# A two-layer FFN and mixer trunk: three pairs of hidden chunks per phase as block products, part of their weight sums by adding DMAs

## The chip, the cores and the metric

One core of a Trainium2 chip runs the whole program. The metric is the time of one execution in device microseconds, the median of several. TensorE (PE) multiplies, VectorE (DVE) and ScalarE (ACT) do the elementwise work, GpSimd (POOL) does little here, SyncE (SP) issues most DMAs.

## The reference

Two layers, each with a half-step FFN, a mixer (differential attention beside an mLSTM) and a second half-step FFN, each between two RMSNorms. x is 256 tokens by 1024, the hidden width is 2816. Only the FFN is touched:

```python
def _swiglu(h, w_in, w_out):
    gate, up = jnp.split(h @ w_in, 2, axis=-1)
    return (jax.nn.silu(gate) * up) @ w_out
...
h = _swiglu(_rmsnorm(x, g[0]), ffn_w_in[l, 0], ffn_w_out[l, 0])
x = x + 0.5 * _rmsnorm(h, g[1])
```

So there are six phases, FFN, mixer, FFN, FFN, mixer, FFN, and the four FFN phases multiply 256 x 1024 tokens by 1024 x 5632 weights and 256 x 2816 by 2816 x 1024, in float32.

## The kernel before, in words

**Precision.** A float32 product is made of three matmuls on fp32r operands (`mm3`, L504-508): high by high, high by low, low by high. A weight piece is one DMA of 128 x 2048 (1 MB, `fetch`, L283-289, on SP's queue) and is split in two halves of 128 x 1024: ACT casts the high part, DVE subtracts for the low part (`halved`, L291-301, the rows of L295 and L296). The raw tiles are three buffers and, every fourth time in an FFN, a shared one (wx); the split halves have seven buffers each, and three in ten borrow from another pool (`half_tiles`, L386).

**Chunks.** The hidden width is cut in 11 chunks of 256. An ordinary chunk (step I) takes two weight pieces and, for both token tiles, 4 x 3 matmuls per piece into one PSUM bank; SiLU and gate follow (`ffn_hidden`, L637), the hidden tile is turned by a transposing DMA on SP's queue (`ffn_planes`, L643, `ffn_joined`, L653) and split again (`ffn_hilo`, L675). Its output part (step O, `out_part`) adds into four PSUM banks that stay open over the phase.

**Pairs.** Step P takes two chunks at once (`pair`, from L764): the two token tiles, the two halves of the input rows and the gate and up columns of both chunks make 2 x 2 blocks, and the Strassen-Winograd scheme gets the block product from seven products of 12 matmuls each (`product`, L759-762) where eight would do it directly. The weight side of the seven products P1 to P7 comes from `pair_blocks` (L310-338): besides the four raw blocks b11, b12, b22, b21 it needs b11 + b12, that sum plus b22, b12 + b22, and the first sum plus b21. Each of the four sums is two DVE additions of 128 x 1024 (L322); every product's weights are split in two halves. The running sum sits in two tiles of the mixer, qk and wt (`spare`, L303). The token sums are made by `pair_tokens` (L341-384) in steps S0 to S2; in all phases but the first they start from scaled tokens that `prenorm_half` (L528) left in the same spare tiles.

**The last chunk** (I10) is computed turned (`in_turned`, L730-742, with `token_scales` and `ffn_turned`): weights stationary, tokens moving, so that its hidden layer comes out already turned.

**Order.** STEPS (L37) lists the steps of a phase after chunks 0 and 1: I a chunk's input, P a pair, S token sums, L the load of an output piece, O an output part. The order of the instructions on each engine is made by a scheduler from this order; `after` (L253) adds ties between instructions. At the phase's end ("ending") PE's order is fixed by hand: output parts 8, 9, 10 of token tile 0, then its postnorm, while token tile 1 follows.

Of the kernel before, what the change touches and what calls it, by code (L numbers as in the profile page):

```python
# [25 lines left out]
P = 128  # L26
# [10 lines left out]
STEPS = "I2 L1 S0 O0 I3 L2 S1 O1 S2 P4 L3 O2 L4 O3 I6 L5 O4 I7 L6 O5 P8 L7 O6 L8 O7 I10 L9".split()  # L37
# [22 lines left out]
def _pack(inp):  # L60
# [9 lines left out]
    def ffn(at, l, f):  # L70
        n = w_in[l, f].reshape(2, 4, P, 2, NC_FF, 256).transpose(0, 3, 2, 1, 4, 5)
        a = n.transpose(4, 0, 2, 3, 1, 5).reshape(NC_FF, 2, P, 2048)
        b = w_out[l, f].reshape(NC_FF, 2, P, D).transpose(0, 2, 1, 3).reshape(NC_FF, P, 2048)
        order = [a[0, 0], a[0, 1], a[1, 0], a[1, 1], b[0]]
        for step in STEPS:
            c = int(step[1:])
            if step[0] == "P":
                order += [n[kh, g, :, :, c:c + 2].reshape(P, 2048) for kh, g in ((0, 0), (0, 1), (1, 1), (1, 0))]
# [57 lines left out]
class _Trunk:  # L136
    def __init__(self, tc, a, out, pools):
        self.tc, self.nc, self.a, self.out = tc, tc.nc, a, out
        self.const, self.wr, self.wl, self.wh, self.tr, self.k2, self.k4, self.ded, self.hp, self.sm, self.ps = pools
        self.piece_at = 0  # L140
        self.parts = None
        self.raws, self.four = 0, False
        self.n = 0
        self.turns = []
        self.halves = 0
        self.both = [None, None]
        self.lend = True

# [161 lines left out]
    def pair_blocks(self):  # L310


        def fetch():
            raw = self.fetch()
            return [raw[:, j] for j in range(2)]

        def split(raw):
            return [self.halved(raw[j]) for j in range(2)]

        def add(out, a, b):  # L320
            for j in range(2):
                self.nc.vector.tensor_tensor(out[j], a[j], b[j], op=ALU.add)  # L322
# [12 lines left out]
        w["P2"] = split(b21)  # L335
        w["P3"] = split(b22)
        add(run, run, b21)
        w["P4"] = split(run)
        return w

    def pair_tokens(self, both, kept):  # L341
# [4 lines left out]
        two = self.t2("aT1", (P, 2, 4, P))  # L346
        s, low = two[:, 0], two[:, 1]
# [4 lines left out]
        def g(kh, t):  # L352
            return self.spare()[t][:, kh * 512:kh * 512 + 512].rearrange("p (k n) -> p k n", k=4)
# [150 lines left out]
    def mm3(self, ps, xh, xl, wh, wl, start, stop):  # L504
        mm = self.nc.tensor.matmul
        mm(ps, xh, wh, start=start, stop=False)  # L506
        mm(ps, xh, wl, start=False, stop=False)  # L507
        mm(ps, xl, wh, start=False, stop=stop)  # L508

# [18 lines left out]
    def prenorm_half(self, t, gi, hf):  # L528
# [4 lines left out]
        if gi % 3 == 1:  # L533
            xg = self.t2("xg", (P, 4, P))
        else:
            xg = self.spare()[t][:, hf * 512:hf * 512 + 512].rearrange("p (k n) -> p k n", k=4)
# [142 lines left out]
    def token_scales(self, r):  # L679

        nc = self.nc
        ptr = self.bank_tr((P, NT * P))
        for t in range(NT):
            nc.tensor.transpose(ptr[:, t * P:(t + 1) * P], r[t].broadcast_to([P, P]), self.ident)
        rows = self.const.tile([P, NT * P], F32, tag="rows", bufs=1, name=self.name("rows"))
        nc.scalar.activation(rows, ptr, AF.Copy)
        return rows

    def ffn_block(self, bank, rows):


        nc, n = self.nc, NT * P
        su = self.t2("su", (P, 2, n))
        for i in range(2):
            nc.scalar.activation(su[:, i], bank[i][:, n:2 * n], AF.Copy)
            nc.vector.tensor_tensor(su[:, i], bank[i][:, 0:n], su[:, i], op=ALU.add)
            nc.vector.tensor_tensor(su[:, i], su[:, i], rows, op=ALU.mult)
            if i == 0:
                self.func(su[:, 0], su[:, 0], AF.Silu)
        nc.vector.tensor_tensor(su[:, 1], su[:, 1], su[:, 0], op=ALU.mult)  # L700
        return su[:, 1].rearrange("p (t j) -> p t j", t=NT)

    def ffn_turned(self, banks, rows):


        ops = [self.ffn_operand() for _ in range(NT)]
        for j in range(2):
            h = self.ffn_block(banks[j], rows)
            for t in range(NT):
                self.guards = [self.ffn_hilo(h[:, t], *(v[:, j] for v in ops[t]))]  # L710
        return [[tuple(v[:, j] for v in ops[t]) for j in range(2)] for t in range(NT)]

    def ffn(self, pre, gi_post):
# [9 lines left out]
        def out_part(c, t, h, wo):  # L723
            for hf in range(2):
                for k in range(2):
                    self.mm3(po[t][hf], *h[t][k], *self.cols(wo, 2 * k + hf),
                             start=c == 0 and k == 0, stop=c == NC_FF - 1 and k == 1)

        def in_turned(banks, w, both):


            blocks = [(banks[j][i], slice(i * 256 + j * P, i * 256 + j * P + P)) for j in range(2) for i in range(2)]
            for group, khs in ((blocks, (0,)), (blocks[:2], (1,)), (blocks[2:], (1,))):
                for kh in khs:
                    for b, c in group:
                        for k in range(4):
                            self.nc.tensor.matmul(b, self.cols(w[kh], k)[0][:, c], both[kh][:, k].rearrange("p i t -> p (i t)"),  # L737
                                                  start=kh == 0 and k == 0, stop=False, skip_group_check=True)
                for b, c in group:
                    for kh in khs:  # L740
                        for k in range(4):
                            self.nc.tensor.matmul(b[:, 0:NT * P], self.cols(w[kh], k)[1][:, c], both[kh][:, k, 0:NT].rearrange("p i t -> p (i t)"),  # L742
                                                  start=False, stop=kh == 1 and k == 3, skip_group_check=True)
# [15 lines left out]
        def product(b, x, w, new):  # L759
            for k in range(4):  # L760
                for n, (st, mv) in enumerate(((x[0], 0), (x[0], 1), (x[1], 0))):
                    self.nc.tensor.matmul(b, st[:, k, :], self.cols(w, k)[mv], start=new and k == n == 0,  # L762
                                          stop=k == 3 and n == 2, skip_group_check=True)

        def pair(c):
# [3 lines left out]
            w = self.pair_blocks()  # L769
# [19 lines left out]
            product(b4, s4, w["P3"], False)  # L789
# [5 lines left out]
            product(b3, xT[1][1], w["P4"], False)  # L795
# [7 lines left out]
        def pair_ready(others):  # L803
            c, turned = sent.pop("pair")
            ops = [[self.ffn_operand() for _ in range(NT)] for _ in range(2)]
            for t in range(NT):
                h = self.ffn_joined(turned[t], others)
                others = [self.ffn_hilo(h[:, j], *ops[j][t])[0] for j in range(2)]
# [3 lines left out]
        hs, po, wo, sent = {}, [], {}, {}  # L812
# [50 lines left out]
        both, swap = list(self.both), 0  # L863
        tokens = self.pair_tokens(both, kept)
        for at, step in enumerate(STEPS):
            kind, c = step[0], int(step[1:])
            if kind == "P":
                pair(c)
                swap = 1
            elif kind == "S":  # L870
                sums = next(tokens)
            elif kind == "L":
                if wo.get(c) is None:
                    wo[c] = self.piece()
            elif kind == "I":
                if c == 3:
                    g = self.load_gpost(gi_post)
                    yield "middle"
# [3 lines left out]
                if "pair" in sent and c != END[-1]:  # L882
                    pair_ready([cut])
                for later in STEPS[at + 1:]:
# [3 lines left out]
                if c == END[-1]:  # L888
                    if "pair" in sent:
                        pair_ready([self.cut])  # L890
                    ready(c - 1, [self.cut])
                    break
                pins = [self.bank_pin() if swap else self.bank_tr() for _ in range(NT)]
                swap = 1 - swap
# [3 lines left out]
                chunk(c, pins)  # L898
            else:
# [578 lines left out]
```

## Time and profile before

| what | value |
|---|---|
| median of 3 runs | 940.26 us (939.74 to 940.84) |
| profiled execution | 940.3 us, span 938.5 us |
| DMA: mean, HBM read | 202 GB/s, 177.01 MB |
| share of the weight queue (q1) | 59.1% of 16 engines' span |
| PE on the chain that ended last | 99% |
| first DVE rows of L580 (postnorm) by phase | 173.9, 279.4, 460.5, 636.9, 742.5, 921.7 us |

A row of a group reads: line, engine, operation, written tile<-read tiles, shapes, count | busy us, mean ns of one | idle time of the engine just before, and who ended it. A row of the timeline reads: start, duration, engine, line, operation, count of merged instructions. A row of the windows reads: window, its length, busy us (and count) of PE, PE's weight loads, DVE, ACT and POOL, the granted clock, the DMA share and GB/s. A row of the waits reads: who <- whom: us in total, times, longest.

### The profile page before, as it was taken

What the parts mean: (1) busy time and instruction counts of PE and PEld (TensorE: products, weight loads), DVE (VectorE), ACT (ScalarE), POOL (GpSimd) and SP (SyncE); (2) the same over time, 40 slices, a digit from 0 to 9 for tenths busy, and PEclk for the clock granted to TensorE, in tenths of its full rate; (3) what the DMA queues carried; (4) which work ended last, traced back from release to release, by engine and by line L of the source; (5) the groups of instructions that cost most, each with busy time, mean ns of one, the idle gap of its engine ahead of it and who ended that gap; (6) DMA issues with size and microseconds to landing.
All of it is one profiled execution on the core that took longest, in us unless ns stands there. A gap on an engine that the chain in (4) does not pass through costs nothing.

```text
span 938.5 us, 12082 instructions
## 1 busy us (share of the span) xinstructions
PE 931.4 (99%) x4427; PEld 771.5 (82%) x4427; DVE 775.5 (83%) x1079; ACT 668.4 (71%) x1033; POOL 29.4 (3%) x57
## 2 busy tenths in 40 slices
PE   9999999999999999999999999999999999999997
PEld 7888888888888888888888888888888888888885
DVE  7989797889867899788698987968898588986974
ACT  8967786677856868676587865866778478766862
POOL 2000000000020000000000000000001100000000
PEclk9999999999999999999999999999999999999999
DMA  9957857346362866838468585473554348486531
GB/s 354 342 169 275 251 192 218 119 152 221 138 232 90 303 167 225 303 107 309 121 237 257 172 267 189 155 237 135 189 193 169 146 157 302 148 300 184 186 115 46
DMA packets 69882, 189.34 MB, mean 202 GB/s; under 512 B 45274, under 2 KB 46426, under 8 KB 49086
## 3 DMA queue, kind: packets, MB, share of 16 engines
q1 hardware_dynamic: 69246, 187.95, 59.1%
q8 instruction: 35, 0.57, 0.2%
q10 hardware_dynamic: 576, 0.61, 0.2%
q14 instruction: 25, 0.20, 0.1%
HBM read 177.01 MB, written 1.05 MB: 190 GB/s over the span
## 4 chain that ended last, share of the span: by engine, by line
PE 99%; DVE 0%; ACT 0%; POOLq 0%; DVEq 0%; issue 0%; ACTq 0%
PE pin L506 11%; PE pin L508 10%; PE pin L507 10%; PE bk L506 10%; PE bk L507 10%; PE bk L508 10%; PE ptr L762 9%; PE pin L762 7%; PE ptr L507 3%; PE ptr L506 3%; PE ptr L508 3%; PE ptr L737 2%; PE pin L737 2%; PE ptr L532 1%; PE ptr L1100 1%; PE pin L742 1%
## 5 line engine op out<-in xcount | busy, mean ns | idle before, releaser
L296 DVE TENSOR_TENSOR wl<-wr,wh 128x1024 fp32r<-128x1024 f32 x262 | 313.6, 1221 | 42.2 <-ACT wh L295 39.4
L295 ACT ACTIVATE wh<-wr 128x1024 fp32r<-128x1024 f32 x262 | 269.5, 1055 | 55.9 <-PE bk L508 15.8
L506 PE MATMUL pin<-wh,both 128*128 128x512 f32 x432 | 171.3, 399 | 0.0
L507 PE MATMUL pin<-wl,both 128*128 128x512 f32 x432 | 168.4, 390 | 0.0
L508 PE MATMUL pin<-wh,both 128*128 128x512 f32 x432 | 168.2, 390 | 0.0
L507 PE MATMUL bk<-wl,hh 128*128 128x512 f32 x352 | 136.3, 389 | 0.0
L506 PE MATMUL bk<-wh,hh 128*128 128x512 f32 x352 | 135.8, 390 | 0.0
L508 PE MATMUL bk<-wh,hl 128*128 128x512 f32 x352 | 133.4, 389 | 0.0
L508 PEld LDWEIGHTS pin<-wh,both 128*128 128x128 f32 x432 | 81.1, 188 | 17.4
L506 PEld LDWEIGHTS pin<-wh,both 128*128 128x128 f32 x432 | 81.3, 188 | 17.2 <-issue 0.7
L507 PEld LDWEIGHTS pin<-wl,both 128*128 128x128 f32 x432 | 81.3, 188 | 15.5
L295 ACT ACTIVATE wh<-wx 128x1024 fp32r<-128x1024 f32 x62 | 64.3, 1055 | 31.9 <-PE bk L508 10.2
L762 PE MATMUL ptr<-wh,both 128*128 128x512 f32 x256 | 84.0, 389 | 0.0
L296 DVE TENSOR_TENSOR wl<-wx,wh 128x1024 fp32r<-128x1024 f32 x62 | 74.7, 1220 | 10.2 <-ACT wh L295 9.5
L508 PEld LDWEIGHTS bk<-wh,hl 128*128 128x128 f32 x352 | 66.1, 188 | 13.8
L506 PEld LDWEIGHTS bk<-wh,hh 128*128 128x128 f32 x352 | 66.1, 188 | 13.5
L507 PEld LDWEIGHTS bk<-wl,hh 128*128 128x128 f32 x352 | 66.1, 188 | 13.4
L762 PE MATMUL pin<-wh,both 128*128 128x512 f32 x192 | 63.0, 389 | 0.0
L762 PEld LDWEIGHTS ptr<-wh,both 128*128 128x128 f32 x256 | 48.0, 188 | 10.0
L507 PE MATMUL ptr<-wl,both 128*128 128x512 f32 x128 | 49.8, 389 | 0.0
L508 PE MATMUL ptr<-wh,both 128*128 128x512 f32 x128 | 49.8, 389 | 0.0
L762 PE MATMUL ptr<-wl,both 128*128 128x512 f32 x128 | 49.8, 389 | 0.0
(263 smaller groups left out, 1464.2 us busy)
## 6 DMA issues: line engine op xcount, KB each, us to landing
wr<-in_w_dram SPq DMA_DIRECT2D x131, 1024.0 KB, 5.1
wx<-in_w_dram SPq DMA_DIRECT2D x31, 1024.0 KB, 5.0
gpost<-in_gpost_dram SPq DMA_DIRECT2D x6, 512.0 KB, 6.2
wr<-in_w_dram SPq DMA_DIRECT2D x2, 512.0 KB, 6.3
wr<-in_w_dram SPq DMA_DIRECT2D x3, 256.0 KB, 4.5
x<-in_x_dram SPq DMA_DIRECT2D x3, 256.0 KB, 5.2
h<-planes SPq DMA_TRANSPOSE x32, 3.3
out_dram<-x SPq DMA_DIRECT2D x2, 256.0 KB, 2.1
```

The costliest lines, as they stand in the source:

```text
L295: ia = nc.scalar.activation(hi, raw, AF.Copy)
L296: iv = nc.vector.tensor_tensor(lo, raw, hi.bitcast(F32), op=ALU.subtract)
L506: mm(ps, xh, wh, start=start, stop=False)
L507: mm(ps, xh, wl, start=False, stop=False)
L508: mm(ps, xl, wh, start=False, stop=stop)
L532: nc.tensor.transpose(ptr[:, k, :], x[:, (4 * hf + k) * P:(4 * hf + k + 1) * P], self.ident)
L737: self.nc.tensor.matmul(b, self.cols(w[kh], k)[0][:, c], both[kh][:, k].rearrange("p i t -> p (i t)"), start=kh == 0 and k == 0, stop=Fals ...
L742: self.nc.tensor.matmul(b[:, 0:NT * P], self.cols(w[kh], k)[1][:, c], both[kh][:, k, 0:NT].rearrange("p i t -> p (i t)"), start=False, sto ...
L762: self.nc.tensor.matmul(b, st[:, k, :], self.cols(w, k)[mv], start=new and k == n == 0, stop=k == 3 and n == 2, skip_group_check=True)
L1100: self.T(ptr[:, b, :], a[:, b * P:(b + 1) * P], self.tr.ident)
```

## The change

- A phase after the first now runs chunks 0, 1, 2, 5 and 8 as ordinary ones and the pairs 3+4, 6+7 and 9+10. The first phase runs chunks 0 to 3 and 6 to 8 as ordinary ones and the pairs 4+5 and 9+10. The turned form of the last chunk and its helpers are gone.
- A new step D starts a pair's first sum: GpSimd's queue copies b12 into the run tile and then adds b11 to it from HBM by an accumulating DMA, 2 x 512 KB each. Inside such a pair, b22 is added to the raw b12 tile in the same way. DVE keeps the other two sums. The pair 4+5 of the first phase has no D and keeps all four on DVE. A pair's pieces come in the order b12, b11, b22, b21.
- The run tiles are the spare ones for the D3 and D9 pairs and the scaled-token tiles for P6. The scaled tokens move to two other tiles: that of aT1, and the one that otherwise holds the post-norm gains. So the gains are loaded in a step of their own (G0), after P6.
- Token tile 1 of the output part three below a pair in the list (O6), and all of O7, are tied to come after the pair's last product. O7 moves to the phase's end. Product P4 is tied to come after P3.
- In the first phase the mixer's constants ("middle") are loaded after chunk 6; they were loaded before chunk 3.

```diff
-STEPS = "I2 L1 S0 O0 I3 L2 S1 O1 S2 P4 L3 O2 L4 O3 I6 L5 O4 I7 L6 O5 P8 L7 O6 L8 O7 I10 L9".split()
+FIRST_STEPS = "I2 L1 S0 O0 I3 L2 S1 O1 S2 P4 L3 O2 D9 L4 O3 I6 L5 O4 I7 L6 O5 G0 I8 L7 P9 L8 O6 L9".split()
+STEPS = "D3 I2 L1 S0 O0 S1 L2 O1 S2 D6 P3 L3 O2 D9 I5 L4 O3 P6 G0 L5 O4 L6 O5 I8 L7 P9 L8 O6 L9".split()
...
+    def by_dma(self, out, i, add=False):
+        for j, v in enumerate(out):
+            self.nc.gpsimd.dma_start(v, self.a["w"][i][:, j * 1024:j * 1024 + 1024], **(dict(accum_op=ALU.add) if add else {}))
+
-    def pair_blocks(self):
+    def pair_blocks(self, run):
...
-        b11, b12 = fetch(), fetch()
+        b12 = fetch()
+        if run:
+            self.by_dma(b12, self.piece_at + 1, True)
+        b11 = fetch()
         w = {"P1": split(b11)}
-        run = self.spare()
-        add(run, b11, b12)
+        summed = run is not None
+        if not summed:
+            run = self.spare()
+            add(run, b11, b12)
         w["P5"] = split(run)
         b22 = fetch()
         add(run, run, b22)
         w["P6"] = split(run)
-        add(b12, b12, b22)
+        if not summed:
+            add(b12, b12, b22)
         w["P7"] = split(b12)
...
+    def scaled_tile(self, t):
+        if t == 0:
+            return self.t2("aT1", (P, 1024))
+        return self.const.tile([P, 1024], F32, tag="gpost", bufs=1, name=self.name("xgt"))
...
-    def in_turned(banks, w, both):
...
+            elif kind == "D":
+                runs[c] = [v for v in self.scaled] if c == 6 else self.spare()
+                i = self.piece_at + sum({"P": 4, "I": 2, "L": wo.get(int(v[1:])) is None}.get(v[0], 0)
+                                        for v in steps[at + 1:steps.index(f"P{c}")])
+                self.by_dma(runs[c], i)
+                self.by_dma(runs[c], i + 1, True)
+            elif kind == "G":
+                g = self.load_gpost(gi_post)
...
-                pins = [self.bank_pin() if swap else self.bank_tr() for _ in range(NT)]
-                swap = 1 - swap
+                pins = [self.bank_tr() if c in (2, 7) else self.bank_pin() for _ in range(NT)]
...
-                    out_part(c, t, hs[c], wo[c])
-        rows = self.token_scales(r)
-        banks = [[self.bank_pin() for _ in range(2)], [self.bank_tr() for _ in range(2)]]
-        in_turned(banks, ws, both)
+                    out_part(c, t, hs[c], wo[c], ended.get(c + 3, []) if t else [])
+        wo[END[-1]] = self.piece()
+        pair_ready([self.cut])
 
         yield "ending"
-        with self.tc.high_priority():
-            hs[END[-1]] = self.ffn_turned(banks, rows)
-        wo[END[-1]] = self.piece()
+        for t in range(NT):
+            out_part(END[0] - 1, t, hs[END[0] - 1], wo[END[0] - 1], ended[END[0] + 1])
```

More of the change, by code (lines that the diff above doesn't have):

```diff
@@ L74, in ffn @@
         order = [a[0, 0], a[0, 1], a[1, 0], a[1, 1], b[0]]
-        for step in STEPS:
+        for step in STEPS if l or f else FIRST_STEPS:
             c = int(step[1:])
             if step[0] == "P":
-                order += [n[kh, g, :, :, c:c + 2].reshape(P, 2048) for kh, g in ((0, 0), (0, 1), (1, 1), (1, 0))]
+                order += [n[kh, g, :, :, c:c + 2].reshape(P, 2048) for kh, g in ((0, 1), (0, 0), (1, 1), (1, 0))]
             elif step[0] in "IL":
@@ L147, in __init__ @@
         self.lend = True
+        self.scaled = [None] * NT
     def name(self, s):
@@ L345, in pair_tokens @@
         tiles = [self.tr.tile([P, 4, 2 * NT, P], F32R, tag="both", name=self.name("both")) for _ in range(2)]
-        two = self.t2("aT1", (P, 2, 4, P))
-        s, low = two[:, 0], two[:, 1]
+        s = self.t2("aT0", (P, 4, P))
+        low = None if kept else self.t2("aT1", (P, 4, P))
         def a(kh, t, lo):
@@ L505, in mm3 @@
         mm = self.nc.tensor.matmul
-        mm(ps, xh, wh, start=start, stop=False)
+        first = mm(ps, xh, wh, start=start, stop=False)
         mm(ps, xh, wl, start=False, stop=False)
         mm(ps, xl, wh, start=False, stop=stop)
+        return first
     def operand(self, part, t, new):
@@ L677, in ffn_hilo @@
         return ia, self.nc.vector.tensor_tensor(hl, h, hh.bitcast(F32), op=ALU.subtract)
[L679 to L711, printed above, removed]
     def ffn(self, pre, gi_post):
@@ L721, in in_piece, with out_part @@
                          start=kh == 0 and k == 0, stop=kh == 1 and k == 3)
-        def out_part(c, t, h, wo):
+        def out_part(c, t, h, wo, behind=()):
             for hf in range(2):
                 for k in range(2):
-                    self.mm3(po[t][hf], *h[t][k], *self.cols(wo, 2 * k + hf),
-                             start=c == 0 and k == 0, stop=c == NC_FF - 1 and k == 1)
-        def in_turned(banks, w, both):
[L732 to L743, printed above, removed]
+                    i = self.mm3(po[t][hf], *h[t][k], *self.cols(wo, 2 * k + hf),
+                                 start=c == 0 and k == 0, stop=c == NC_FF - 1 and k == 1)
+                    self.after(i, behind)
         def send(c, h):
@@ L757, in chunk, with product @@
             ready(c - 1, i[:1])
-        def product(b, x, w, new):
+        def product(b, x, w, new, behind=()):
             for k in range(4):
                 for n, (st, mv) in enumerate(((x[0], 0), (x[0], 1), (x[1], 0))):
-                    self.nc.tensor.matmul(b, st[:, k, :], self.cols(w, k)[mv], start=new and k == n == 0,
-                                          stop=k == 3 and n == 2, skip_group_check=True)
+                    i = self.nc.tensor.matmul(b, st[:, k, :], self.cols(w, k)[mv], start=new and k == n == 0,
+                                              stop=k == 3 and n == 2, skip_group_check=True)
+                    self.after(i, behind)
+            return i
         def pair(c):
             tt, stt = self.nc.vector.tensor_tensor, self.nc.vector.scalar_tensor_tensor
-            w = self.pair_blocks()
+            w = self.pair_blocks(runs.pop(c, None))
             b1, b2, b3, b4 = self.bank_pin(), self.bank_pin(), self.bank_tr(), self.bank_tr()
@@ L788, in pair @@
                 self.func(sil, b1, AF.Silu, scale=r[0])
-            product(b4, s4, w["P3"], False)
+            i = product(b4, s4, w["P3"], False)
             with ahead():
@@ L807, in pair_ready @@
                 h = self.ffn_joined(turned[t], others)
-                others = [self.ffn_hilo(h[:, j], *ops[j][t])[0] for j in range(2)]
+                pairs = [self.ffn_hilo(h[:, j], *ops[j][t]) for j in range(2)]
+                others = [p[0] for p in pairs]
+                if t == 0:
+                    self.guards = pairs[1:]
             for j in range(2):
                 hs[c + j] = self.ffn_pairs(ops[j])
-        hs, po, wo, sent = {}, [], {}, {}
+        hs, po, wo, sent, runs, ended = {}, [], {}, {}, {}, {}
         kept = bool(xT)
@@ L862, in ffn @@
             ready(0, [i])
-        both, swap = list(self.both), 0
+        both = list(self.both)
         tokens = self.pair_tokens(both, kept)
-        for at, step in enumerate(STEPS):
+        steps = STEPS if kept else FIRST_STEPS
+        for at, step in enumerate(steps):
             kind, c = step[0], int(step[1:])
@@ L881, in ffn @@
                 ws.append(self.piece())
-                if "pair" in sent and c != END[-1]:
+                if "pair" in sent:
                     pair_ready([cut])
-                for later in STEPS[at + 1:]:
+                for later in steps[at + 1:]:
                     if later[0] != "L":
```

19 lines of the change are left out of this document (7 added, 12 removed).

## The prediction

> **What bounds the kernel now.** I read the page's busy table first, then what TensorE (PE) waited for, then its timeline, and last the busy time by stage.
>
> ```profile
> span 938.5 us, 12082 instructions
> PE 931.4 (99%) x4427; PEld 771.5 (82%) x4427; DVE 775.5 (83%) x1079; ACT 668.4 (71%) x1033; POOL 29.4 (3%) x57
> PEclk9999999999999999999999999999999999999999
> ...
> PE bk L495 <- PEq L1468: 0.8, 1, 0.8
> ```
>
> PE is busy 99% at full clock, and over the whole span it waited once, 0.8 us, for its own start. But a busy share of PE proves little where matmuls overlap, so I look at when they start, in one stretch of 24 alike (first and last row):
>
> ```profile
> 183.27 0.39 PE L506 MATMUL pin<-wh,both 128*128 128x512 f32 x1
> ...
> 188.48 0.39 PE L508 MATMUL pin<-wh,both 128*128 128x512 f32 x1
> ```
>
> Each row lasts 0.39 us, yet 24 starts span 5.21 us: (188.48 - 183.27) / 23 = 0.2265 us. This pitch, not the 0.39, is what one 512-column matmul costs. PE starts one every pitch and waits for nobody: the time is the number of matmuls times the pitch, with a short head and tail. So every matmul saved is saved in full, and everything else in this change matters only if it makes PE wait.
>
> **What the change takes from PE.** The last chunk (10) now runs in the turned form of L730-742, which starts at 441.25 in this phase and is followed by the next output part at 452.63:
>
> ```profile
> 441.25 1.98 PE L737 MATMUL pin<-both,wh 128*128 128x512 f32 x8
> 443.06 0.75 PE L742 MATMUL pin<-both,wl 128*128 128x256 f32 x5
> 443.65 0.38 PE L684 MATMUL ptr<-c,rs 128*128 128x128 f32 x2
> ...
> 452.63 0.40 PE L506 MATMUL bk<-wh,hh 128*128 128x512 f32 x1
> ```
>
> That is 11.38 us for one chunk (32 wide and 32 half-wide matmuls and two transposes), 45.5 for the four FFN phases. It goes altogether. What comes in its place is counted from the code. An ordinary chunk takes 2 x 2 x 4 x 3 = 48 matmuls, a pair 7 products x 12 = 84. A phase outside the turned chunk has six chunks and two pairs now, 6 x 48 + 2 x 84 = 456. The first phase gets seven chunks and two pairs, 504, that is 48 more; each of the other three gets five chunks and three pairs, 492, 36 more. Output parts stay as they are. Added: (48 + 3 x 36) x 0.2265 = 156 x 0.2265 = 35.3 us. Sum on PE: 35.3 - 45.5 = -10.2 us, of which -0.5 in the first phase and -3.2 in each later one. The profiled execution took 940.3 us (span 938.5 and 1.8 around it), the median of the runs is 940.26, so they stand for each other: 940.3 - 10.2 = **930.1 us if PE still never waits**.
>
> **What has to stay hidden: VectorE (DVE) and ScalarE (ACT).** Means of one instruction, and the stage between two postnorms as a window (the second FFN phase), with a short window in which DMA runs flat out:
>
> ```profile
> 292.00:460.00 168.00, 168.00 (x763) 139.82 (x762) 139.35 (x170) 120.75 (x160) 1.63 (x3) 1.00 0.64 215
> 380.00:390.00 10.00, 10.00 (x45) 8.27 (x45) 5.89 (x8) 7.34 (x10) 0.00 (x0) 1.00 1.07 380
> ...
> L296 DVE TENSOR_TENSOR wl<-wr,wh 128x1024 fp32r<-128x1024 f32 x262 | 313.6, 1221 | 42.2 <-ACT wh L295 39.4 <-PE bk L508 1.5 <-ACT sil L267 0.8
> L322 DVE TENSOR_TENSOR wt<-wt,wr 128x1024 f32<-128x1024 f32 x14 | 17.1, 1219 | 0.0
> L677 DVE TENSOR_TENSOR hl<-hT,hh 128x256 fp32r<-128x256 f32 x80 | 31.2, 419 | 15.6 <-ACT hh L676 15.6
> L677 DVE TENSOR_TENSOR hl<-su,hh 128x128 fp32r<-128x128 f32 x16 | 4.2, 289 | 7.0 <-ACT hh L676 7.0
> L640 DVE SCALAR_TENSOR_TENSOR h<-pin,rs,sil 128x256 f32<-128x256 f32 x30 | 14.2, 478 | 2.6 <-ACT sil L267 2.6
> L697 DVE TENSOR_TENSOR su<-su,rows 128x256 f32<-128x256 f32 x16 | 6.6, 421 | 0.2
> L797 DVE TENSOR_TENSOR u<-ptr,u 128x512 f32<-128x512 f32 x8 | 5.5, 686 | 0.0
> L799 DVE SCALAR_TENSOR_TENSOR v<-v,rs,u 128x512 f32<-128x512 f32 x8 | 6.0, 745 | 0.0
> ```
>
> DVE in a later phase. A pair has 14 halves to split where two chunks had 8: +6 x 1.22 = +7.3. The sums fall from 2 pairs x 8 halves to 3 x 4: -4 x 1.22 = -4.9. One more pair is read out, five additions and two scaled ones: 5 x 0.69 + 2 x 0.75 = +4.9; one plain chunk less, 2 x 0.48 = -1.0. Turned chunk: eight operations on su, 8 x 0.42, and four short splits, 4 x 0.29 = -4.5; its 256-wide replacement +2 x 0.42 = +0.8. Together +2.6: 139.4 becomes 142 of 168 - 3.2 = 164.8 us, 86% after 83%.
>
> ```profile
> L295 ACT ACTIVATE wh<-wr 128x1024 fp32r<-128x1024 f32 x262 | 269.5, 1055 | 55.9 <-PE bk L508 15.8 <-PE ptr L762 12.3 <-PE pin L508 8.3
> L656 ACT ACTIVATE hT<-h 128x1024 uint16<-128x1024 uint16 x32 | 43.7, 1364 | 7.0 <-DMA h<-planes 7.0
> L648 ACT ACTIVATE planes<-h 128x1024 uint16<-128x1024 uint16 x32 | 33.6, 1050 | 17.5 <-DVE h L640 17.5
> L676 ACT ACTIVATE hh<-hT 128x256 fp32r<-128x256 f32 x80 | 29.0, 409 | 0.3
> L267 ACT ACTIVATE u<-u,rs 128x512 f32<-128x512 f32 x8 | 5.7, 707 | 0.0
> ```
>
> ACT, without taking off what the turned chunk cost it: six casts 6.3, one more plane, turn and two hh 3.2, three 512-wide read-outs at no more than 0.71, 2.1: 120.8 + 11.6 = 132 of 164.8, 80%. Neither engine becomes the bound on average, so I cost both at nothing, the cover being PE's unbroken row of matmuls.
>
> The average hides the pairs themselves. The second pair of that phase began at 411.33 and the next output part followed its last product at 438.30:
>
> ```profile
> 411.33 0.39 PE L762 MATMUL pin<-wh,both 128*128 128x512 f32 x1
> ...
> 438.07 0.39 PE L762 MATMUL ptr<-wh,both 128*128 128x512 f32 x1
> 438.30 0.39 PE L506 MATMUL bk<-wh,hh 128*128 128x512 f32 x1
> ...
> 411.00:438.00 27.00, 27.00 (x121) 22.37 (x120) 23.76 (x25) 21.70 (x26) 0.00 (x0) 1.00 0.67 223
> ```
>
> 26.97 us, or 119 pitches, for 84 products: some 35 matmuls of output parts (7.9 us) were slipped in between while the weights were being split. With four additions less per pair DVE comes 4.9 us sooner, so a pair wants about 3.0 us of filling. The first two pairs have whole output parts around them (24 x 0.2265 = 5.4 us each). The last has little: the second token tile of O6, and all of O7, are now tied behind its end, and only 12 matmuls, 2.7 us, are left. I charge 0.3 us for each of four last pairs, +1.2.
>
> Behind that last pair the tied work is the cover for its hidden layer. For token tile 0 the chain is two DVE operations, planes, the transposing DMA, turn, hh, hl: 0.69 + 0.75 + 1.05 + 3.3 + 1.36 + 0.41 + 0.42 = 8.0 us; PE has meanwhile the last product, half of O6, O7 and half of O8, 60 x 0.2265 = 13.6 us. Without it PE would wait those 8 us four times.
>
> ```profile
> wr<-in_w_dram SPq DMA_DIRECT2D x131, 1024.0 KB, 5.1
> h<-planes SPq DMA_TRANSPOSE x32, 3.3
> ...
> SPq L288 <- DVE wl L296: 557.5, 123, 15.7
> POOL rs L521 <- DVE s L560: 487.2, 18, 163.6
> ```
>
> **Queues and DMA.** SP's queue stood 557.5 us waiting for raw tiles that DVE had not split: it is fed by buffers, not by bandwidth. The later gain load (G0) waits on it for the split of P6's last sum; behind it stand the next weight loads, which mostly wait for that same stretch of DVE, so nothing is charged. The sums move to GpSimd's queue, six half-megabyte DMAs for each pair that has a D step. A waiting addition there holds up only later DMAs and the small powers of L521, and GpSimd is idle but for 29 us.
>
> No adding DMA is in the trace. Flat out, DMA moved 380 GB/s, so a plain 1.05 MB costs 2.76 us of all engines: the low end. The high end is the only other DMA that is not a plain load, the transposing one: 256 KB in 3.3 us, 13.2 us for a megabyte. I take the plain load as the nearer row (the same bytes and long rows from the same array). A later phase uses 0.64 x 168 = 107.5 us of DMA; nine more megabytes make 132, 80% of 164.8. The bound is reached when an addition costs (164.8 - 107.5 - 3 x 2.76) / 6 = 8.2 us.
>
> The Trainium skill speaks against this part: in "Collectives: The Full Stack", section "The bandwidth ceiling", an addition inside a DMA reads two sources for each write and reached about half the rate of a copy (ratio 1.93). By that rule six of the nine megabytes count twice, an estimate of 149 of 164.8 us, which still lies under the bound and leaves the sum where it is. No trace of before can show it.
>
> **The rivals.**
> *The last pair starves.* DVE arrives at it just in time, after two dense pairs, and the filling has been used up ahead of it. It loses half of the 3.0 us in each of four phases and some in the others, about 6 us: 936. If all of the 3.0 is lost four times, 12 us: 942. For: the filling is tied away; three pairs now follow close. Against: DVE was idle 3.2 us of the 27 in that window.
> *The adding DMAs are the bound, slower than before.* Each microsecond that an addition takes above 8.2 costs 6 us per later phase, 18 us in all; at 9.2 it is 948, and the gain is gone at 8.8. For: half of the way from 2.76 to 13.2 lies about there. Against: the D copies and their additions are issued ahead of their pair, so only the third addition is due at once.
> *GpSimd's queue holds back a norm.* A D copy that waits for its buffer stands ahead of the power that gives a phase its scale; the first read-outs then wait about one landing, 5.1 us, three times: 945. Against: those buffers are free long before a phase begins.
> *The saving is not there.* If turned matmuls and products only traded places, PE would show it in the count; the starts above leave no room for that, and I give it nothing.
>
> **How the numbers follow.** No waits on PE beyond the 1.2 us: 0.70, at 930.1 + 1.2 = 931.3. Starved last pair: 0.14 at 936, 0.04 at 942. DMA bound: 0.08 at 948 or more. GpSimd: 0.04 at 945. A measurement of this kernel tells about 0.2%, 1.9 us, from no change: faster is below 938.4, which holds 0.84; 942 is the same, 0.04; the other two are slower, 0.12. The range goes from 929.5 (930.1 less half of the 1.1 us by which the runs of before differ) to 938.4 and takes in the first two cases.
>
> **What would show it.** Right: no L737 or L742 rows, 156 more 512-wide matmuls, PE's list of waits still near nothing, its pitch 0.2265, DVE near 86% of a later phase, the additions landing in under 8 us. Wrong: PE waiting for wl or wh inside the third pair (starved), DVE waiting for the summed tiles with a DMA share near 1 (DMA bound), or PE waiting at a phase's start behind L521.

## The result and the profile after

The changed kernel is slower: 1015.92 us median (1004.45 to 1017.51, 6 runs) against 940.32 before, ratio 1.0778 with an interval of 1.0729 to 1.0827. The forecast was 931.3. The profiled execution took 1010.9 us, its span is 1009.0.

The page of the changed kernel: busy times, PE's clock, GpSimd's DMA queue (packets, MB, share of 16 engines), and the engines' shares of the chain that ended last.

```profile
span 1009.0 us, 12077 instructions
PE 943.8 (94%) x4319; PEld 767.9 (76%) x4319; DVE 776.7 (77%) x1050; ACT 687.9 (68%) x1028; POOL 76.2 (8%) x117
PEclk9999999999999998998999899799999999979989
q0 software_dynamic: 8640, 31.46, 14.9%
PE 53%; DMA 15%; DVE 10%; issue 4%; ACT 2%; DVEq 0%; POOLq 0%; ACTq 0%
```

The matmul count fell as forecast: 4319 after 4427, which is 156 added and 264 taken away. But PE no longer starts one every pitch. The chain that ended last was all PE before; now 15% of it is DMA and 10% DVE. The clock row, unbroken before, has dips.

What PE waited for, and the wait of ACT that has grown most (same columns: total, times, longest):

```profile
PE ptr L736 <- DVE v L761: 17.6, 4, 7.4
PE ptr L736 <- ACT wh L297: 16.4, 8, 8.4
PE pin L736 <- ACT wh L297: 12.5, 1, 12.5
PE bk L526 <- ACT hh L699: 7.0, 4, 4.5
...
ACT hT L679 <- DMA h<-planes: 44.7, 8, 15.2
```

PE waited 0.8 us before and 58 us now, nearly all of it at the pairs' products (L736) or at an output part behind them (L526). ACT waited 44.7 us for transposing DMAs to land, where it had waited 7.0 before (the row of L656). The groups of transposing DMAs, first before, then after, show it from the other side:

```profile
DMA to landing us min/median/max: 3.0/3.7/7.6
```

```profile
DMA to landing us min/median/max: 3.0/5.4/24.4
```

The longest single wait, in the third FFN phase, shows how it goes. First the queues (SP's transposes, GpSimd's additions into aT and xgt, ACT's next instruction), then the windows:

```profile
532.34 12.77 SPq L673 DMA_TRANSPOSE h<-planes  x2
...
534.72 0.87 POOL L321 DMA_DIRECT2D aT<-in_w_dram  x1 [9.28 <-DMA aT<-in_w_dram]
538.35 0.86 POOL L321 DMA_DIRECT2D xgt<-in_w_dram  x1 [2.76 <-DMA xgt<-in_w_dram]
...
540.51 1.06 ACT L297 ACTIVATE wh<-wx 128x1024 fp32r<-128x1024 f32 x1
556.80 1.34 ACT L679 ACTIVATE hT<-h 128x1024 uint16<-128x1024 uint16 x1 [15.23 <-DMA h<-planes]
...
535.00:540.00 5.00, 5.00 (x24) 4.14 (x23) 5.00 (x7) 5.00 (x8) 1.45 (x2) 1.00 1.01 397
545.00:550.00 5.00, 1.58 (x7) 0.96 (x6) 1.00 (x1) 0.00 (x0) 0.00 (x0) 1.00 1.22 81
550.00:555.00 5.00, 0.00 (x0) 0.00 (x0) 0.00 (x0) 0.00 (x0) 0.00 (x0) 0.55 1.36 55
560.00:565.00 5.00, 5.00 (x15) 3.86 (x15) 5.00 (x8) 5.00 (x7) 0.55 (x1) 0.59 0.35 103
```

Two transposes and two additions are in flight together. DMA falls from 397 to 55 GB/s while its share stands above 1: the engines count as full and move almost nothing. ACT's next instruction wants the first transposed tile, so every cast behind it stands 15.23 us. DVE runs out of casts to subtract, PE out of weights. And when PE goes on, it does so at 0.59 of its clock, 15 matmuls in 5 us where there were 24.

### The profile page after: what moved, and what is told of

Its sections match the earlier page's. It is cut to its first block, busy times and chain, and to the rows that moved or that the text cites. A ratio compares the mean times of both kernels' runs of the same rounds, so it can differ in the third digit from the quotient of the medians.

```text
span 1009.0 us, 12077 instructions
## 1 busy us (share of the span) xinstructions
PE 943.8 (94%) x4319; PEld 767.9 (76%) x4319; DVE 776.7 (77%) x1050; ACT 687.9 (68%) x1028; POOL 76.2 (8%) x117
## 4 chain that ended last, share of the span: by engine, by line
PE 53%; DMA 15%; DVE 10%; issue 4%; ACT 2%; DVEq 0%; POOLq 0%; ACTq 0%
DMA h<-planes 12%; PE bk L526 7%; PE bk L527 7%; PE pin L526 6%; DVE wl L298 6%; PE bk L528 6%; PE pin L528 6%; PE pin L527 6%; PE ptr L736 5%; PE pin L736 3%; DMA wr<-in_w_dram 3%; ACT wh L297 1%; DMA wx<-in_w_dram 1%; PE ptr L1078 1%; PE ptr L553 1%
## 5 line engine op out<-in xcount | busy, mean ns | idle before, releaser
L298 DVE TENSOR_TENSOR wl<-wr,wh 128x1024 fp32r<-128x1024 f32 x262 | 314.7, 1220 | 71.2 <-ACT wh L297 69.3
L526 PE MATMUL pin<-wh,both 128*128 128x512 f32 x448 | 177.2, 398 | 0.0
L528 PE MATMUL pin<-wh,both 128*128 128x512 f32 x448 | 174.8, 390 | 0.0
L527 PE MATMUL pin<-wl,both 128*128 128x512 f32 x448 | 174.6, 390 | 0.0
L736 PE MATMUL ptr<-wh,both 128*128 128x512 f32 x352 | 124.5, 418 | 34.1 <-DVE v L761 17.6
L526 PE MATMUL bk<-wh,hh 128*128 128x512 f32 x352 | 138.5, 397 | 7.0 <-ACT hh L699 7.0
L528 PE MATMUL bk<-wh,hl 128*128 128x512 f32 x352 | 129.8, 389 | 0.0
L736 PEld LDWEIGHTS ptr<-wh,both 128*128 128x128 f32 x352 | 71.3, 202 | 54.9 <-ACT wh L297 20.5
L736 PE MATMUL pin<-wh,both 128*128 128x512 f32 x264 | 87.0, 392 | 12.6 <-ACT wh L297 12.5
L528 PEld LDWEIGHTS pin<-wh,both 128*128 128x128 f32 x448 | 84.1, 188 | 18.0
L526 PEld LDWEIGHTS pin<-wh,both 128*128 128x128 f32 x448 | 84.3, 188 | 17.6 <-issue 0.7
L527 PEld LDWEIGHTS pin<-wl,both 128*128 128x128 f32 x448 | 84.3, 188 | 16.2
L298 DVE TENSOR_TENSOR wl<-wx,wh 128x1024 fp32r<-128x1024 f32 x62 | 74.5, 1220 | 17.7 <-ACT wh L297 17.6
L526 PEld LDWEIGHTS bk<-wh,hh 128*128 128x128 f32 x352 | 67.3, 191 | 22.5 <-ACT hh L699 8.3
L528 PEld LDWEIGHTS bk<-wh,hl 128*128 128x128 f32 x352 | 66.1, 188 | 13.7
L736 PE MATMUL ptr<-wl,both 128*128 128x512 f32 x176 | 73.6, 418 | 2.4 <-DVE wl L298 2.4
L679 ACT ACTIVATE hT<-h 128x1024 uint16<-128x1024 uint16 x33 | 44.8, 1357 | 44.7 <-DMA h<-planes 44.7
L736 PEld LDWEIGHTS pin<-wh,both 128*128 128x128 f32 x264 | 49.7, 188 | 24.1 <-ACT wh L297 13.7
## 6 DMA issues: line engine op xcount, KB each, us to landing
xgt<-in_w_dram POOLq DMA_DIRECT2D x6, 512.0 KB, 13.7
```

What stands on the lines that cost most here:

```text
L298: iv = nc.vector.tensor_tensor(lo, raw, hi.bitcast(F32), op=ALU.subtract)
L526: first = mm(ps, xh, wh, start=start, stop=False)
L679: i = self.nc.scalar.activation(hT.rearrange("p a b n -> p (a b n)").bitcast(U16).rearrange("p (n u) -> p u n", u=2), turned.rearrange("p ...
L736: i = self.nc.tensor.matmul(b, st[:, k, :], self.cols(w, k)[mv], start=new and k == n == 0, stop=k == 3 and n == 2, skip_group_check=True)
```

## The experiments

My first theory was this meeting of adding and transposing DMAs. Rivals were the queue or the bytes as such, and the prediction's own rival, a last pair that starves.

**Copies for additions.** Same instructions in the same order; sums left out.

```diff
-**(dict(accum_op=ALU.add) if add else {})
+**{}
```

> The adding DMAs are made plain copies of the same bytes on the same queue, in the same instruction order; the sums they should make are left out, so b12 + b22 is b22 and b11 + b12 is b11. My theory (an adding DMA and a transposing DMA in flight together hold each other up, and ACT stands behind the late transposing DMA): no transposing DMA lands later than 9 us, PE waits under 10 us in all, the time is 930 to 940 us. Rival 1 (any DMA of GpSimd's queue does it, or the bytes as such): time stays above 975 us with transposing DMAs of 14 us and more. Rival 2 (three pairs starve PE whatever moves the sums): time above 960 us with transposing DMAs that land in time.

Measured: 976.35 us, ratio 1.0383 (1.0343 to 1.0422). Neither side had it: 40 us go with the additions, some 45 over the 931.3 stay. The theory's own signs were missed too: transposes landed after up to 13.4 us (24.4 in the changed kernel), and PE waited 30 us in all. GpSimd's queue moved the same bytes:

```profile
q0 software_dynamic: 8640, 31.46, 9.8%
...
PE ptr L736 <- DVE v L761: 14.4, 4, 5.3
...
ACT hT L679 <- DMA h<-planes: 15.1, 7, 3.8
```

So ACT's wait fell from 44.7 to 15.1 us, while PE's wait for v (17.6 us, longest 7.4) stayed at 14.4, longest 5.3. That one has another cause.

**All sums on DVE**, no step D, no DMA on GpSimd's queue (the lists lose D3, D6 and D9):

> No step D: three pairs per later phase as in the change, all four sums of every pair on DVE, no DMA on GpSimd's queue. My theory: transposing DMAs land in 3 to 8 us as before the change; PE's matmuls cost 930 us; DVE has 14.6 us more to do per later phase, some 157 of 165 us, so PE waits a little: 932 to 950 us. Rival 2 (three pairs starve PE): over 960 us with PE waiting for wl and wh inside the pairs.

Measured: 969.79 us, ratio 1.0315 (1.0276 to 1.0354). Transposes land in 3.0 to 7.5 us, as the theory had it, but the time is above its 950. Without any adding DMA 39 us over 931 remain, and PE waits for v and wl of the pairs:

```profile
PE ptr L736 <- DVE v L761: 17.1, 4, 6.2
PE pin L736 <- DVE wl L298: 7.7, 5, 2.1
```

**One addition by DMA in the kernel before.**

```diff
         add(run, b11, b12)
+        for j in range(2):
+            self.nc.gpsimd.dma_start(b12[j], self.a["w"][self.piece_at][:, j * 1024:j * 1024 + 1024], accum_op=ALU.add)
...
-        add(b12, b12, b22)
```

> The kernel before, two pairs per phase and the turned last chunk, with only b12 + b22 moved from DVE to an adding DMA on GpSimd's queue. My theory: the adding DMAs meet the transposing DMA of the chunk before or of the pair and slow it to 10 us and more wherever they meet: 945 to 985 us although DVE has 2.4 us less to do per pair. Rival 2 (the three pairs are the cause): 938 to 942 us.

Measured: 940.64 us, ratio 1.0002 (0.9991 to 1.0012). A miss for the theory as I had put it. Transposes did land later, up to 9.9 us, and PE waited 0.8 us in all, as before:

```profile
DMA to landing us min/median/max: 3.0/4.1/9.9
```

So the meetings of this version, with two additions to a pair instead of four, cost nothing: PE had other work throughout. That a meeting costs time only where PE has nothing else to do is my reading; it was not tried apart.

**The DMAs by themselves**, seven stages (neither FFN nor mixer is computed):

```diff
+stages = (lambda: turn(), lambda: move(nc.gpsimd, sums, True), lambda: move(nc.gpsimd, sums, False),
+          lambda: (move(nc.gpsimd, sums, True), turn()), lambda: (move(nc.gpsimd, sums, False), turn()),
+          lambda: (move(nc.scalar, raws, False), turn()), lambda: (move(nc.gpsimd, sums, True), move(nc.scalar, raws, False)))
```

> No FFN and no mixer: seven stages of DMAs alone, the output is zeros. Stages: six transposing DMAs; eight adding DMAs of 512 KB; eight copies of 512 KB on GpSimd's queue; adding with transposing; copies on GpSimd's queue with transposing; copies on ACT's queue with transposing; adding beside copies on ACT's queue. My theory: the fourth stage takes far longer than the first and second together (at least 1.5 times), the fifth, sixth and seventh no longer than their parts one after the other. Rival 1 (GpSimd's queue as such): the fifth is stretched as well. If it is bytes alone, no stage is longer than the sum of its parts.

The windows cut at the stages, from one run (window, length, busy DVE and POOL, clock, DMA share, GB/s):

```profile
26.80:37.10 10.30, 3.20 (x22) 0.00 (x0) 1.00 0.80 153
37.70:61.70 24.00, 1.68 (x12) 7.17 (x8) 1.00 0.93 175
63.90:78.10 14.20, 1.61 (x12) 4.26 (x8) 1.00 0.80 295
78.10:132.80 54.70, 2.93 (x22) 7.02 (x8) 1.00 1.14 105
132.80:156.20 23.40, 3.10 (x24) 4.28 (x8) 1.00 0.88 247
156.20:184.00 27.80, 4.61 (x33) 0.00 (x0) 1.00 0.99 208
184.00:218.50 34.50, 2.08 (x14) 7.00 (x8) 1.00 0.97 244
```

Six transposes alone take 10.3 us, eight additions 24.0, eight copies 14.2. The windows of the last four stages begin with 0.7 to 2.0 us in which DVE still reads the tiles of the stage before; counted from their first DMA they take 52.9, 21.4, 25.9 and 33.8 us. So additions with transposes take 1.5 times the 34.3 of both one after the other; copies with transposes less than their 24.5; additions beside copies from ACT's queue also less than their parts, if a copy there costs what it does on GpSimd's queue. Copies from ACT's queue with transposes are a little over theirs, a small miss. It is adding and transposing together, in no kernel's order, and by the margin expected.

**No transposing DMA**: plain ones of the same bytes; the turning is left out, the additions stay.

```diff
-nc.sync.dma_start_transpose(turned, planes.rearrange("p u n -> p (u n)"))
+nc.sync.dma_start(turned.rearrange("p b n -> p (b n)"), planes.rearrange("p u n -> p (u n)"))
```

> The changed kernel with every transposing DMA replaced by a plain one of the same 256 KB on the same queue; the hidden tiles stay unturned, so the turning itself is left out. All adding DMAs stay. If adding and transposing DMAs hold each other up only together, the replaced ones land within 6 us, ACT no longer waits for them (44.7 us in the changed kernel falls under 15) and the time falls by 30 to 40 us to 970 to 980 us. If the adding DMAs alone cost it (by the bytes, or late sums), the time stays above 1000 us.

Measured: 983.68 us, ratio 1.0458 (1.0437 to 1.0479), 32 us less, and so 4 us above the 970 to 980. The plain DMAs landed after up to 16.2 us (median 5.1), not within 6. ACT's wait falls from 44.7 to 13.7:

```profile
ACT hT L679 <- DMA h<-planes: 13.7, 4, 4.5
```

Taking either partner away gives back 32 to 40 us, and each figure holds what that partner costs by itself. Against the 969.79 us of the version with all sums on DVE, copies beside transposes cost 6.6 us, additions without transposes 13.9, both together 46.1. So some 26 us belong to neither alone, if plain DMAs in the place of transposes gain nothing by themselves; that was not run.

**Kept apart by waits** between GpSimd's additions and SP's transposes (`self.apart` makes the first wait for the second; the lists hold the last two of each kind):

```diff
+            if add:
+                self.apart(d, self.turning)
+                self.adding = (self.adding + [d])[-2:]
...
+        self.apart(d, self.adding)
+        self.turning = (self.turning + [d])[-2:]
```

> The changed kernel with waits that keep them apart: an adding DMA waits for the last transposing DMAs before it, a transposing DMA for the last adding DMAs before it. Theory (the two in flight together): each transposing DMA, once issued, lands in under 6 us, and the time falls below the 1011 us of the changed kernel, but not down to the 976 us of the version with copies, as the waits themselves delay: 975 to 1005 us. If the overlap is not the cause, the added waits only cost: above 1015 us.

Measured: 1062.23 us, ratio 1.1294 (1.1271 to 1.1316). The transposes land in time, 7.3 us at most, but the waiting transpose holds SP's queue, and behind it the weight loads:

```profile
DMA to landing us min/median/max: 3.0/3.7/7.3
...
SPq L683 <- DMA wt<-in_w_dram: 83.7, 7, 13.3
ACT wh L304 <- DMA wr<-in_w_dram: 94.4, 25, 10.6
```

By its own terms the expectation fell on the side against the theory (above 1015). It missed what a wait costs everything queued behind it, the fault of the prediction once more; with the weight loads held up as well, this run decides nothing on the overlap.

**Only the first sum by DMA**: b12 + b22 is back on DVE.

```diff
-        if run:
-            self.by_dma(b12, self.piece_at + 1, True)
...
-        if not summed:
-            add(b12, b12, b22)
+        add(b12, b12, b22)
```

> The changed kernel, but b12 + b22 back on DVE; only the first sum of each pair (step D) is made by DMA. Half of the adding bytes remain, and those are issued ahead of the pair. If the harm comes from each meeting of an adding and a transposing DMA: about half of the 35 us goes, less 3 us or so for DVE's four more additions per pair: 985 to 1005 us. If the urgent b12 + b22 alone was to blame: 968 to 980 us.

Measured: 992.6 us, ratio 1.0553 (1.047 to 1.0637), about midway, though its two runs lie 13 us apart (985.89 and 999.3): the harm is not that of the urgent addition alone.

**The same sums on GpSimd itself** (`self.nc.gpsimd.tensor_tensor` for b11 + b12 and b12 + b22, no step D):

> Three pairs as in the change; b11 + b12 and b12 + b22 are added by GpSimd itself (four 128x1024 additions per pair), no DMA on its queue. DVE has the same load as in the change, the DMAs are those of the version with all sums on DVE. If the 970 us of that version came from DVE's load, this one falls towards 945 us; if it came from the last pair, behind whose end the remaining output parts are tied, PE still waits 5 to 8 us there in each phase: 955 to 970 us. If GpSimd's additions take over 4 us each they are late themselves and the time is above 975 us.

Measured: 1014.55 us, ratio 1.0786 (1.0764 to 1.0808). Each addition takes 3 us, under the 4 I had set as the limit, and four in a row take 12 us:

```profile
L336 POOL TENSOR_TENSOR wr<-wr,wx 128x1024 f32<-128x1024 f32 x14 | 43.9, 3155 | 8.7 <-DMA wx<-in_w_dram 8.7
```

But DVE did not have the load I had expected. Beside these additions its own work slowed down: the splits of wr take 1320 ns instead of 1220, those of wx 1474 instead of 1219, and DVE is busy for 857.0 us where it had 818.8 with all sums on DVE and 44 operations more. So this version tells nothing of DVE's load as the cause, and it does not separate late additions from a slower DVE.

For the second cause, what costs 39 us without any addition by DMA, I separated the place of the last pair from the third pair.

**Two pairs, the second at the end**: all phases run the first phase's list, all sums on DVE.

```diff
-        steps = STEPS if kept else FIRST_STEPS
+        steps = FIRST_STEPS
```

> All phases run the first phase's list: two pairs, the second of them with the last chunk, all sums on DVE, no turned chunk. PE's matmuls: four times 0.5 us less than before, 938 us. If the last pair's place at the end is what starves, PE waits some 5 us in it, at half clock for some time after, in every phase: 955 to 970 us. If the density of three pairs is the cause: 938 to 942 us.

Measured: 968.49 us, ratio 1.0296 (1.0273 to 1.032).

**The last chunk ordinary**: the kernel before with chunk 10 as a plain one and O7 behind it.

```diff
-... P8 L7 O6 L8 O7 I10 L9
+... P8 L7 O6 L8 I10 O7 L9
```

> The kernel before, two pairs at 4+5 and 8+9 and all sums on DVE, but the last chunk as an ordinary one instead of turned, with O7 behind it. PE's matmuls cost 0.5 us less per phase: 938.3 us. If the loss of the version with two pairs (968 us) comes from the last chunks being a pair, this one takes 937 to 945 us. If it comes from giving up the turned chunk as a cover that needs no transposing DMA, PE waits for hh at the end of each phase, 5 us and more: 955 to 970 us.

Measured: 939.3 us (938.3 to 940.43, 10 runs), ratio 0.9988 (0.9978 to 0.9997), PE unbroken. Pages of these two, two pairs at the end first:

```profile
span 968.3 us, 11922 instructions
PE 943.6 (97%) x4355; PEld 773.1 (80%) x4355; DVE 767.4 (79%) x1039; ACT 672.2 (69%) x1013; POOL 29.4 (3%) x57
```

```profile
span 936.2 us, 11899 instructions
PE 928.7 (99%) x4355; PEld 766.5 (82%) x4355; DVE 764.0 (82%) x1039; ACT 670.6 (72%) x1013; POOL 29.4 (3%) x57
```

Every engine has the same number of busy instructions, and the medians differ by 29 us. What differs is the place of the second pair, the order around it and the ties behind it, and also the change's other edits, which the first version keeps, among them the tie of P4 behind P3, the order of a pair's pieces, the tiles of the scaled tokens, the later gain load and the PSUM banks. That the last pair is where the time goes, its trace shows: apart from 0.8 us at its start, all of PE's waits lie in the last pairs of the four phases. In that of the second FFN phase PE stops like this (PE's waits over the span, its rows, then DVE's, then windows):

```profile
PE ptr L736 <- DVE v L761: 9.1, 4, 3.5
PE pin L736 <- DVE wl L298: 7.5, 5, 2.4
...
447.41 0.39 PE L736 MATMUL pin<-wh,both 128*128 128x512 f32 x1
451.32 0.80 PE L736 MATMUL ptr<-wh,both 128*128 128x512 f32 x1 [3.52 <-DVE v L761]
...
447.72 0.67 DVE L760 TENSOR_TENSOR v<-u,ptr 128x512 f32<-128x512 f32 x1
448.32 1.21 DVE L298 TENSOR_TENSOR wl<-wr,wh 128x1024 fp32r<-128x1024 f32 x1
449.45 1.21 DVE L298 TENSOR_TENSOR wl<-qk,wh 128x1024 fp32r<-128x1024 f32 x1
450.59 0.67 DVE L761 TENSOR_TENSOR v<-v,ptr 128x512 f32<-128x512 f32 x1
...
447.00:452.00 5.00, 1.48 (x6) 0.91 (x5) 5.00 (x7) 3.96 (x5) 0.00 (x0) 0.77 0.92 338
452.00:462.00 10.00, 10.00 (x36) 8.05 (x35) 6.71 (x8) 4.86 (x6) 0.00 (x0) 0.77 0.25 75
```

Product P3 adds into a bank that DVE must read first (L761), and DVE, busy 5.00 of 5 us, is still splitting. PE has no output part to slip in. Then it runs at 0.77 of its clock: 36 matmuls in the 10 us that hold 44 at the pitch of 0.2265. DVE's order has a share in the stop: what L761 reads was there when L760 ended, at 448.39, but two splits stand ahead of it, so that some 2.2 of the 3.52 us are that order, an estimate from these rows.

**Untied**: three pairs, all sums on DVE, O6 and O7 free to fill the last pair (`ended` no longer passed on, O7 ahead of the end).

> The version with all sums on DVE, without the ties behind the last pair: O6 and O7 may fill it, and nothing but half of O8 is kept for its end. Theory starved (the last pair lacks filling): the waits of 4 to 6 us inside the last pair go, but the hidden layer of the last pair (a chain of 8 us) is now uncovered at the end, so the waits move there: 950 to 970 us, with PE waiting for hh in the last output parts. Rival (three dense pairs as such): the waits inside the pairs stay and the time is 965 us or more.

Measured: 970.2 us, ratio 1.0314 (1.0294 to 1.0335), as it was with the ties. The time is that of the rival, the waits are those of the theory: they moved to the end, to the hidden layer that has lost its cover:

```profile
PE bk L526 <- ACT hh L699: 19.8, 6, 6.7
```

**More filling**: the version with two pairs at the end, O5 placed behind the last pair.

```diff
-... L6 O5 G0 I8 L7 P9 L8 O6 L9
+... L6 G0 I8 L7 P9 O5 L8 O6 L9
```

> The version with two pairs, the second at the end with the last chunk (968 us), with the steps O5 and P9 exchanged: one more output part, 24 matmuls or 5.4 us, may be slipped into the last pair; DVE's work is the same. If that pair starves for want of filling, its waits of 3 to 4 us and part of the half-clock time behind them go: 940 to 955 us. If filling is not what it lacks, 965 us or more.

Measured: 962.93 us, ratio 1.0242 (1.0212 to 1.0272). Between the two bounds: 5.6 us in all come back with 5.4 us of filling in each of the four phases. Want of filling is a part; one output part of it does not bring back the 29 us.

**Three pairs elsewhere**, in three versions. First the kernel before with pairs 2+3, 5+6, 8+9 and the turned last chunk, b12 + b22 by an adding DMA; then the same pairs with the plain last chunk and all sums on DVE; then that with b12 + b22 on GpSimd. The list shown is that of the last two; the first has O7 I10 at its end.

```diff
+STEPS = "S0 L1 O0 S1 S2 P2 L2 O1 I4 L3 O2 L4 O3 P5 L5 O4 I7 L6 O5 L7 O6 P8 L8 I10 O7 L9".split()
```

> The kernel before with a third pair: in the later phases the pairs 2+3, 5+6, 8+9 and the turned last chunk as before; b12 + b22 of every pair by an adding DMA, the other three sums on DVE; nothing is tied behind the last pair. PE's matmuls: 12 less in three phases, 940.3 - 3 x 12 x 0.2265 = 932 us. If the place of the last pair is what costs, this one has the turned chunk to fill and to cover it and takes 932 to 937 us. If three pairs are too dense for DVE (some 153 of 165 us), PE waits inside the pairs: above 945 us.

> The version with the plain last chunk, and a third pair in the later phases: pairs 2+3, 5+6, 8+9, the ordinary chunk 10 last, all sums on DVE, no DMA on GpSimd's queue, nothing tied. PE's matmuls are those of the changed kernel, 930 us. If only the place of the last pair was to blame (beside the adding DMAs), this one takes 930 to 936 us and beats both. If three pairs are too dense for DVE, whose load is some 96% of a later phase here, PE waits inside the pairs in all of the three later phases: above 945 us.

> The same with b12 + b22 added by GpSimd itself, two additions of 3.1 us per pair, DVE relieved of 7.3 us per later phase. If density on DVE is the cause, it lies some 10 us or more below the version without; if GpSimd's additions come late for P7, above it.

Measured: 1017.55 us (ratio 1.0809, 1.0746 to 1.0873), 1004.21 (1.0679, 1.0659 to 1.07) and 1019.4 (1.0846, 1.0811 to 1.088). All three far from 932. The second phase of FFN in the version with all sums on DVE, postnorm to postnorm (length, busy PE, PEld, DVE, ACT and POOL, clock, DMA share, GB/s), and what PE waited for most in that version:

```profile
278.60:483.50 204.90, 188.41 (x800) 151.29 (x799) 165.67 (x191) 136.01 (x176) 2.18 (x4) 0.97 0.54 181
...
PE bk L507 <- ACT hh L677: 27.1, 17, 5.0
```

The same stretch of before is 184.0 us long, PE busy throughout. DVE has 165.7 us to do where PE's work would leave about 180, so its sum alone would fit. PE's longest waits are at output parts, for hidden layers that come late (L677), 27.1 us against 12.1 inside the pairs, so that density of DVE in the pairs is not shown as the cause. The version with GpSimd does not decide it either: DVE is busy 840.3 us there against 820.4, with 22 operations fewer. A pair directly after the token sums, with DVE not yet ahead, may add to it; that wasn't tried apart.

## Why the prediction was wrong

*PE's count and pitch: right.* 4319 matmuls as counted, and the version with a plain last chunk, which takes off 2.0 us of matmuls and leaves PE unbroken, came out at 939.3 where the count gave 938.3. The 930.1 us stand as a floor by the count; no version with 4319 matmuls came near them.

*DVE's load: right in size, wrong as an argument.* The forecast was 2.6 us more per later phase; by windows from postnorm to postnorm, before and after, it is 152.4 after 150.4. The mean of 86% hid where the load falls.

```profile
278.00:462.00 184.00, 184.00 (x839) 153.14 (x838) 150.36 (x184) 129.47 (x177) 2.19 (x4) 1.00 0.60 200
...
286.70:488.20 201.50, 183.74 (x794) 148.80 (x793) 152.41 (x179) 134.74 (x172) 16.10 (x22) 0.97 0.81 236
```

*The term that failed first: "I charge 0.3 us for each of four last pairs, +1.2."* It was the rival "the last pair starves" that I priced at 6 to 12 us and gave 0.18. The last pair in its place, with the change's other edits around it, costs 29 us with two pairs and the same number of instructions (968.49 less 939.30); PE waits 4 us in it per phase where I had charged 0.3. I took the filling that the second pair of before had used and set 2.7 us against 3.0; but that pair also had O6, O7 and the turned chunk at hand, some 22 us of matmuls that want less of DVE than a pair does, and the same work covered the hidden layer behind it. The turned chunk, which I counted as 11.4 us to be saved, was cover as well. Its form does not matter, for an ordinary chunk in its place covers just so (939.3 us); a chunk and two output parts behind the pair are what the last pair lacks.

*The term that failed second: "I take the plain load as the nearer row".* Adding DMAs by themselves take 24.0 us for eight, 6.0 per megabyte where the sum had 2.76. That is still below the 8.2 at which I let the rival begin. The share of 0.81 in the row above looks like my 80%, but it is of a phase of 201.5 us: 163 us of DMA after 110 (0.60 of 184.0), 53 us more where I had added 25. And what an addition met was not asked: the transposing DMA of the chunk before, on which ACT stands with all its casts. Together they take 1.5 times their sum, and taking either away is worth 32 to 40 us of the loss. The rule of the Trainium skill ("Collectives: The Full Stack", "The bandwidth ceiling"), stated there for collectives, has an addition at about half the rate of a copy. It agrees roughly for additions alone: 24.0 against 14.2 us is a factor of 1.7, where it has 1.93. It does not speak of transposes.

*What was left out: the clock.* No term said that a stop of PE costs more than its length. In the profiled run of the version with two pairs at the end the waits add up to 18 us, while its span is 32 us longer than that of the plain last chunk (968.3 and 936.2). Its mean granted clock is 0.984 against 0.998, which is 13.6 us of PE's time, some 11 of them outside the waits: together 29 of the 32 us. In the changed kernel the same working gives 58 us of waits and some 16 of slower clock (0.969). The Trainium skill has it in "TensorE: Matmul & The Clock Gate", "Part 1: The HAM clock gate", a gate that falls to half speed after about 3.4 us of idling and opens again after as long of work. The traces agree on the half: behind the wait of 3.52 us the clock is 0.50 for the first 5.2 us, in which PE starts 12 matmuls instead of 23, and then 1.00. They do not agree on the 3.4 us, for shorter stops did it too: after 2.06 us (all sums on DVE, at 811.2) and after 1.78 us (three pairs elsewhere, at 510.8) the clock was 0.50 for some 3.4 us.

*GpSimd's queue and the later gain load: held.* No wait of PE goes back to L542 or to the gains.

Along one path the medians share the loss out: the plain last chunk 939.3; less 36 matmuls in three phases, 8.2 us, 931.1; the last pair at the end +29.2; the third pair, sums on DVE, +9.5 (969.79 less 968.49, and the 8.2); the sums' traffic as copies on GpSimd's queue +6.6, although DVE is relieved; additions in place of copies +39.6; together 1015.9. The first steps come from different lists, so this is one order of taking them and not the only one. Open are: why adding and transposing DMAs hold each other up; how much of the 29 us is filling, how much cover, how much DVE's order and how much the change's other edits (the ties were lifted and the filling raised, neither the order on DVE nor those edits were changed by themselves); why the third pair and the copies cost what they do; and whether three pairs could be spaced to fit at all. No version tried here with three pairs beats the kernel before; the plain last chunk with two pairs does, by 0.03 to 0.22%, which counts as the same.

## What to carry to other kernels

When PE never waits, count its matmuls for the gain, but price every other edit by what stands next to it at that place: the mean load of an engine over a phase says nothing of a dense step at the phase's end, where the work that filled its gaps has just been removed. Before moving work to a DMA, list what else is in flight then and which in-order queue waits for that. And count a stop of PE at more than its length.

## What the runs showed of the hardware that was not expected

An adding DMA alone costs 6.0 us per megabyte against 3.6 for a copy on the same queue (24.0 and 14.2 us for eight of 512 KB). Beside transposing DMAs, both crawl: 52.9 us for what takes 34.3 in turn, 55 GB/s in the worst window of the kernel at a DMA share of 1.36. Copies do not do this (21.4 us together, 24.5 in turn). Behind many of its stops PE runs at half its clock for some microseconds: 12 matmuls in 5.2 us instead of 23 after a stop of 3.52 us, and the same clock of 0.50 after stops as short as 1.78 us. GpSimd adds two 128x1024 float32 tiles in 3.16 us, against 1.22 on DVE, and DVE gets slower beside it: 1.32 and 1.47 us for splits that take 1.22.
